# Two blocks' attention probabilities transposed in f32 where they are made, and the last gate product issued behind the first mixed rows

## The chip, the cores and the metric

The kernel runs on one core of one Trainium2 chip. The metric is the device time of one execution in microseconds (us); lower is better. The engines are called as the profile calls them: PE is TensorE (matmuls; PEld its weight loads), DVE is VectorE, ACT is ScalarE, POOL is GpSimd, and SP is the queue from which most DMAs are issued. Each engine runs its own instructions in order, and waits on semaphores for the others.

## The reference

One layer of a hybrid backbone over 2048 latent tokens of width 1024, with 256 context tokens. Cut to what matters here:

```python
def sink_softmax(logits, sink):
    m = jnp.maximum(jnp.max(logits, axis=-1, keepdims=True), sink)
    p = jnp.exp(logits - m)
    return p / (jnp.sum(p, axis=-1, keepdims=True) + jnp.exp(sink - m))
...
    h = rms_norm(x) * (1.0 + scale[:, None, :]) + shift[:, None, :]
    rq, rk, rv, rg, aq, ak, av, ag = project(h, w_in[l])
...
    ret_x, _, _ = retention_branch(rq, rk, rv, rg, log_gamma, ret_gn_w[l], s_fwd, s_bwd)
    att_x = merge_heads(windowed_gqa(aq, ak, av, cak, cav, att_sink[l])) * jax.nn.silu(ag)
    mixed = jnp.concatenate([ret_x, att_x], axis=-1) @ w_out[l]
    x = x + gate[:, None, :] * mixed
    return rms_norm(x) * final_norm_w
```

Retention has 4 heads of 128, in both directions, with a group norm and a SiLU gate (rg). Attention has 8 heads of 64 on 2 key/value heads: a block of 128 queries sees its own and the two neighbouring blocks of 128 keys and all 256 context keys, so a row of probabilities has 640 entries, 512 in the first and the last block, and one for the sink behind them.

## The kernel before

It has two phases. The first, up to about 688 us, makes all projections: for groups of 512 tokens, products of the weights and the normalised input, each split in a high and a low fp32r half (three products a tile). The last chunk is ag1 of the first token group (the rows "ag" of L343). The second phase goes over 16 blocks of 128 tokens, two steps a block (one for each key/value head, kv), 32 steps t in all. A step holds attention heads of the next step, retention, transposes and products of the present one, and pieces of the output projection. The tables STEPS, FIRST and WEAVE give the order in which the program writes them; a scheduler then orders each engine's instructions by its own estimate of when their inputs are there, in a window around that. `behind(i)` binds an instruction to come after instruction i. The first block's heads are woven into the last gate chunk by WEAVE (0 to 7 are heads, A and B the first transposes, a and b their products), and FIRST has what follows in step 0: its transposes T, the mixed rows Y (`ret_out`), and G (`last_gate`).

One attention head goes like this. PE makes the scores S (L759 and L763; there is one buffer for S, so the next head's scores wait until it is read). DVE adds the mask and takes the maximum (L767), puts the sink's column behind (L772) and prepares the bias (L773). ACT takes the exponential with the sum (L776). DVE takes the reciprocal of the sum (L785), POOL multiplies by it (L786). These work on a tile p of 641 columns, of which there are four, shared by all steps. Then SP issues a DMA that copies the row from p into tile pr (L790). pr holds the four heads of a step in fp32r, 640 columns each, and there are two of them.

For each 128 keys (kt), PE transposes the four heads of pr (L1200) against identr, the identity in fp32r, into a bank pt. ACT rounds pt to the high half phl (L1206), DVE subtracts for the low half (L1207), and PE multiplies both with the values into o (L1217). Block 0 has four kt, the others five, so a step has 16 or 20 transposes.

`gate_by_tanh` (L1233 to L1236) makes a gate: tanh on ACT, a scale by 0.5 on DVE or POOL, the product with the projection on DVE (L1235, tile gl), and a DMA to memory. `ret_out` (L1274 to L1279) transposes the retention rows (yt, against ident, the identity in f32), multiplies by the gate gr (L1276), and splits the result in mr, a cast (a helper's line, L113) and a subtraction (L1279); block 0 does both on DVE, the others on POOL. `proj` (L1290) is the output projection pz, from mr (weights wg0) and from the attention's rows ma (weights wg1).

Loads are issued on SP in the order of the program. Of these, `load_qkv` and `load_late` (tile xb) come behind the latest pr copy from block 2 on:

```python
            with behind(PE["copy"] if b > 1 else None):
                nc.sync.dma_start(QKV[b], d_qkv[b])
```

Of the kernel before, what the change touches and what calls it, by code (L numbers as in the profile page):

```python
# [8 lines left out]
F32 = mybir.dt.float32  # L9
F32R = mybir.dt.float32r  # L10
# [29 lines left out]
def tile_hymba(  # L40
# [49 lines left out]
    sink8 = const.tile([P, 8], F32, name="sink8")  # L90

    EPSV = (EPS, EPS * P)
    half4 = const.tile([P, 4], F32, name="half4")
    dve.memset(half4, -0.5)
    eps1 = const.tile([P, 1], F32, name="eps1")
    dve.memset(eps1, EPS)


# [589 lines left out]
    def load_qkv(b):  # L688
        if b < NB:
            QKV[b] = l2.tile([P, 3, RH, P], F32, tag="qkv", name=f"qkv{b}")  # L690
            with behind(PE["copy"] if b > 1 else None):
                nc.sync.dma_start(QKV[b], d_qkv[b])

    def load_st(b):
# [33 lines left out]
    def load_late(b):  # L728
        if b >= NB:
            return  # L730
        tiles_late(b)
        if b:
            nc.sync.dma_start(GA[b], d_g[b, :, 1])
        else:
            nc.sync.dma_start(GA[b][:, 0:2], d_g[b, :, 1, 0:2])
        with behind(PE["copy"] if b > 1 else None):
            nc.sync.dma_start(XB[b], xn[b * P : (b + 1) * P, :])


    def att_head(b, kv, j):  # L740
        slots = window(b)[0]
        nl = len(slots) * P
        n = nl + CTX
        o = 512 - nl
        h = 4 * kv + j
        ksel = {0: slice(0, 2), NB - 1: slice(0, 3, 2)}.get(b, slice(0, 3))
        m0 = mask_at(b)
        mk = C2["msk"][:, m0 : m0 + n // P].rearrange("p s t -> p (s t)")
        if j == 0:
            PB[(b, kv)] = (  # L750
                C2["pool"].tile([P, 4, 640], F32R, tag="pr", name=f"pr{b}_{kv}"),
                C2["pool"].tile([P, 3, 4], F32, tag="m4", name=f"m4{b}_{kv}"),
                [C2["pool"].tile([P, 641], F32, tag="pb", name=f"p{b}_{kv}_{i}", bufs=4) for i in range(4)],
            )
        _, m4, pbs = PB[(b, kv)]
        pb = pbs[j]
        psc = pS.tile([P, 1024], F32, tag="S", name=f"S{b}_{h}")
        for hl in range(2):
            i = pe.matmul(  # L759
                psc[:, o:512].rearrange("p (s t) -> p s t", t=P),  # L760
                AQ[b][:, h, :], C2["kwin"][:, kv, hl, ksel], start=(hl == 0), stop=(hl == 1),
            )
            pe.matmul(psc[:, 512:768], AQ[b][:, h, :], C2["kctx"][:, kv, hl], start=(hl == 0), stop=(hl == 1))  # L763
        PE["S"] = i

        with behind(PE["low"] if (b, kv) == (1, 0) else None):
            i = PE["max"] = dve.tensor_tensor_reduce(  # L767
                out=pb[:, 0:n], in0=psc[:, o : o + n], in1=mk, op0=ALU.add, op1=ALU.max,
                scale=1.0, scalar=-3e38, accum_out=m4[:, 0, j : j + 1],
            )  # L770
        with behind(i):
            dve.tensor_copy(pb[:, n : n + 1], sink8[:, h : h + 1])  # L772
        dve.tensor_scalar(  # L773
            m4[:, 1, j : j + 1], m4[:, 0, j : j + 1], -0.125, nsink[:, h : h + 1], op0=ALU.mult, op1=ALU.min
        )
        act.activation(  # L776
            pb[:, 0 : n + 1], pb[:, 0 : n + 1], AF.Exp, bias=m4[:, 1, j : j + 1], scale=0.125,
            accum_out=m4[:, 2, j : j + 1],
        )

    def att_norm(b, kv, j):
        n = len(window(b)[0]) * P + CTX
        pr_, m4, pbs = PB[(b, kv)]
        pb = pbs[j]
        dve.reciprocal(m4[:, 2, j : j + 1], m4[:, 2, j : j + 1])  # L785
        PE["norm"] = pool.tensor_scalar(  # L786
            pb[:, 0:n], pb[:, 0:n], m4[:, 2, j : j + 1], 0.0, op0=ALU.mult, op1=ALU.add
        )

        PE["copy"] = nc.sync.dma_start(pr_[:, j, 0:n].bitcast(F32), pb[:, 0:n])  # L790

    BANKS = {"o": 1, "z": 2, "t": 3}

# [400 lines left out]
    def att_t(b, kv, kt, weave=False):  # L1194
# [2 lines left out]

        with behind(PE.get("prod") if kt == 0 else None):
            for j in range(4):
                pe.transpose(ppt[:, j].bitcast(F32R), pb[:, j, kt * P : (kt + 1) * P], identr)  # L1200
        if weave:
            phl = [tmp(f"phl{kt}{x}", dt=F32R).rearrange("p (j t) -> p j t", t=P) for x in "hl"]
        else:
# [27 lines left out]
    def gate_by_tanh(t, idx, ps, eng):  # L1231

        act.activation(t, ps, AF.Tanh, scale=0.5)  # L1233
        eng.tensor_scalar(t, t, 0.5, 0.5, op0=ALU.mult, op1=ALU.add)
        dve.tensor_tensor(t, t, ps, op=ALU.mult)  # L1235
        act.dma_start(d_g[0:4, :, 1, idx, :].rearrange("b d t -> d b t"), t.rearrange("d (b t) -> d b t", b=4))  # L1236


# [31 lines left out]
    def ret_out(b):  # L1270
        sd = RT[b][1]
        pt = bank(f"yt{b}")
        for h in range(RH):
            pe.transpose(pt[:, h], sd[:, h], ident)  # L1274
        g = GR[b]
        dve.tensor_tensor(g, pt, g, op=ALU.mult)  # L1276
        MR[b] = s1.tile([P, 2, RH, P], F32R, tag="mr", name=f"mr{b}")
        rounded(MR[b][:, 0], g, "pool" if b else "dve")
        (pool if b else dve).tensor_tensor(MR[b][:, 1], g, MR[b][:, 0], op=ALU.subtract)  # L1279


    PZ = {}
# [212 lines left out]
```

## Time and profile before

| what | us |
|---|---|
| median of three timed runs | 1150.86 |
| lowest and highest of the three | 1150.78 and 1152.02 |
| the profiled execution, its own time | 1151.28 |
| its span, from the first to the last instruction | 1149.5 |
| mean granted clock of PE | 0.995 of full |
| DMAs pr<-p: count, median from issue to landing | 128 of them; the 112 of 320 KB take 3.0 |

The profile is of one execution. Rows of the timeline have the start, the duration, engine, line, operation, output and inputs, count, and in brackets the idle time ahead and what ended it. Rows of several windows have the window, then for each engine busy time and count, the granted clock (1.00 is full), the share of the DMA engines and GB/s. Buffer numbers are left out of names: pr stands for all pr tiles. Matmuls are pipelined: a row's duration overlaps the next one's, so the distance of two starts tells more than a duration.

### The profile page before, as it was taken

The page shows a single profiled execution, that of the slowest core. Times are in us where ns is not written, and L with a number is a line of the kernel's source. Part 1 is how long each engine was busy: PE and PEld are TensorE (multiplying, and loading weights), DVE is VectorE, ACT ScalarE, POOL GpSimd, SP SyncE. Part 2 cuts the span into 40 slices and gives each one's busy share as a digit, 9 for nine tenths or more (in the row PEclk, how much of TensorE's full clock was granted, in tenths as well). Part 3 has the DMA queues.
Part 4 walks back from the last instruction along what each step waited for, and adds up shares of the span by engine and source line. Part 5 has one row for each costly group of instructions (what it writes and reads, how often), then busy time and mean ns, then how long its engine had stood idle before and what let it go on. Part 6 is the DMA issues. An engine that isn't in the chain of part 4 may idle for free.

```text
span 1149.5 us, 18705 instructions
## 1 busy us (share of the span) xinstructions
PE 1121.1 (98%) x6317; PEld 959.8 (83%) x6318; DVE 800.2 (70%) x2029; ACT 467.6 (41%) x1030; POOL 330.7 (29%) x429
## 2 busy tenths in 40 slices
PE   8999999999999999999999998899999999999997
PEld 5877879989988889998888876788888888888885
DVE  7873994655664555656566456778888888888884
ACT  4444512332443002332111343555556655556563
POOL 0000020100011100002014333455555555555552
PEclk9999999999999999999999999999999999999999
DMA  9948883374675533543356378666666666666541
GB/s 340 335 145 263 296 279 119 120 255 136 203 234 170 146 103 88 170 133 97 115 181 195 94 207 269 199 230 231 227 233 228 228 228 225 228 227 227 188 147 65
DMA packets 158552, 224.32 MB, mean 195 GB/s; under 512 B 13300, under 2 KB 105204, under 8 KB 158327
## 3 DMA queue, kind: packets, MB, share of 16 engines
q1 hardware_dynamic: 142324, 214.95, 57.3%
q10 hardware_dynamic: 16130, 8.16, 2.4%
q8 instruction: 50, 0.82, 0.3%
q14 instruction: 48, 0.39, 0.1%
HBM read 130.13 MB, written 50.86 MB: 157 GB/s over the span
## 4 chain that ended last, share of the span: by engine, by line
PE 80%; DVE 7%; issue 5%; DMA 4%; ACT 2%; POOL 2%; SPq 0%; POOLq 0%; DVEq 0%; ACTq 0%
PE pz L1290 14%; PE ag L343 8%; PE rk L343 7%; PE rv L356 7%; PE o L1217 6%; PE aq L343 5%; PE rg L343 4%; PE S L759 4%; PE rq L343 4%; PE pt L1200 4%; PE S L763 2%; PE av L343 2%; PE ak L343 2%; PE u L472 2%; DVE wss L215 1%
## 5 line engine op out<-in xcount | busy, mean ns | idle before, releaser
L786 POOL TENSOR_SCALAR p<-p,m 128x640 f32<-128x640 f32 (+1 forms) x128 | 107.7, 842 | 107.0 <-DMA kwin<-d_k 46.3
L776 ACT ACTIVATE p<-p,m 128x641 f32<-128x641 f32 (+1 forms) x128 | 104.6, 817 | 75.9 <-DVE m L773 45.8
L1207 DVE TENSOR_TENSOR phl<-pt,phl 128x512 fp32r<-128x512 f32 x154 | 104.7, 681 | 18.7 <-ACT phl L1206 18.4
L767 DVE CUSTOM_DVE_ANT_0 p<-S,msk 128x640 f32<-128x640 f32 (+1 forms) x128 | 102.2, 798 | 10.1 <-PE S L763 6.5
L1206 ACT ACTIVATE phl<-pt 128x512 fp32r<-128x512 f32 x154 | 90.9, 592 | 43.8 <-PE pt L1200 37.7
L1290 PE MATMUL pz<-wg0h,mr 128*128 128x512 f32 x256 | 98.2, 406 | 1.9 <-DVE mr L113 1.9
L1290 PE MATMUL pz<-wg1h,ma 128*128 128x512 f32 x256 | 99.0, 413 | 0.2
L759 PE MATMUL S<-kwin,aq 128*128 128x384 f32 (+1 forms) x256 | 85.1, 352 | 3.1 <-DVE m L767 2.0
L1200 PEld LDWEIGHTS pt<-identr,pr 128*128 128x128 f32 x624 | 68.2, 141 | 15.7 <-DMA pr<-p 3.0
L448 ACT ACTIVATE vw<-v,wdec 128x128 fp32r<-128x128 f32 x128 | 43.7, 394 | 84.8 <-DVE v L461 84.8
L1200 PE MATMUL pt<-identr,pr 128*128 128x128 f32 x624 | 72.2, 240 | 3.3 <-DMA pr<-p 2.8
L1217 PE MATMUL o<-phl,vwin 128*128 128x512 f32 x180 | 72.3, 429 | 2.9 <-DVE phl L1207 2.1
L763 PE MATMUL S<-kctx,aq 128*128 128x256 f32 x256 | 71.4, 282 | 0.0
L1290 PEld LDWEIGHTS pz<-wg0h,mr 128*128 128x128 f32 x256 | 48.0, 188 | 10.4 <-DVE mr L113 2.2
L759 PEld LDWEIGHTS S<-kwin,aq 128*128 128x128 f32 x256 | 48.1, 188 | 7.8 <-DVE m L767 3.0
L1290 PEld LDWEIGHTS pz<-wg1h,ma 128*128 128x128 f32 x256 | 48.0, 188 | 7.8 <-POOL ma L1268 1.0
L763 PEld LDWEIGHTS S<-kctx,aq 128*128 128x128 f32 x256 | 48.4, 189 | 2.7
L1290 PE MATMUL pz<-wg0l,mr 128*128 128x512 f32 x128 | 50.5, 394 | 0.0
L1290 PE MATMUL pz<-wg1l,ma 128*128 128x512 f32 x128 | 50.5, 394 | 0.0
L1261 ACT ACTIVATE ob<-o 64x512 f32<-64x512 f32 x32 | 19.1, 596 | 63.9 <-PE o L1217 63.9
L450 DVE SCALAR_TENSOR_TENSOR vw<-v,wdec,vw 128x128 fp32r<-128x128 f32 x128 | 40.4, 360 | 6.7 <-ACT vw L448 6.7
L1217 PEld LDWEIGHTS o<-phl,vwin 128*128 128x128 f32 x180 | 32.4, 187 | 14.3 <-DVE phl L1207 5.8
(444 smaller groups left out, 3057.2 us busy)
## 6 DMA issues: line engine op xcount, KB each, us to landing
pr<-p SPq DMA_DIRECT2D x112, 320.0 KB, 3.0
wss<-in_wss SPq DMA_DIRECT2D x32, 512.0 KB, 5.9
qkv<-d_qkv SPq DMA_DIRECT2D x15, 768.0 KB, 5.9
aq<-d_aq SPq DMA_DIRECT2D x64, 128.0 KB, 3.2
xb<-in_xn SPq DMA_DIRECT2D x16, 512.0 KB, 4.0
out<-xb SPq DMA_DIRECT2D x31, 256.0 KB, 2.6
st<-d_st SPq DMA_DIRECT2D x15, 512.0 KB, 3.5
d_g<-g ACTq DMA_DIRECT2D x28, 256.0 KB, 2.8
```

Of the source, the lines that this page charges most:

```text
L343: pe.matmul(ps, w[:, a, k, c0 : c0 + P], ht[b][:, k, :], start=(k == 0 and i == 0), stop=(k == NK - 1 and i == 2),)
L356: pe.matmul(ps, ht[a][:, k, t * P : (t + 1) * P], w[:, b, k, :], start=(k == 0 and i == 0), stop=(k == NK - 1 and i == 2),)
L759: i = pe.matmul(psc[:, o:512].rearrange("p (s t) -> p s t", t=P), AQ[b][:, h, :], C2["kwin"][:, kv, hl, ksel], start=(hl == 0), stop=(hl = ...
L763: pe.matmul(psc[:, 512:768], AQ[b][:, h, :], C2["kctx"][:, kv, hl], start=(hl == 0), stop=(hl == 1))
L767: i = PE["max"] = dve.tensor_tensor_reduce(out=pb[:, 0:n], in0=psc[:, o : o + n], in1=mk, op0=ALU.add, op1=ALU.max, scale=1.0, scalar=-3e3 ...
L776: act.activation(pb[:, 0 : n + 1], pb[:, 0 : n + 1], AF.Exp, bias=m4[:, 1, j : j + 1], scale=0.125, accum_out=m4[:, 2, j : j + 1],)
L786: PE["norm"] = pool.tensor_scalar(pb[:, 0:n], pb[:, 0:n], m4[:, 2, j : j + 1], 0.0, op0=ALU.mult, op1=ALU.add)
L1200: pe.transpose(ppt[:, j].bitcast(F32R), pb[:, j, kt * P : (kt + 1) * P], identr)
L1206: PE["phl"] = act.activation(phl[0], ppt, AF.Copy)
L1207: PE["low"] = dve.tensor_tensor(phl[1], ppt, phl[0], op=ALU.subtract)
L1217: pe.matmul(PO[kv], vt, PH[kt][hl], start=(kt == 0 and hl == 0), stop=(kt == nkt - 1 and hl == 1))
L1290: PE["prod"] = pe.matmul(PZ[n2], m[:, a, k % RH, :], WG[k // 4][c][:, k % 4, s], start=(k == 0 and i == 0), stop=(k == NK - 1 and i == 2),)
```

## The change

There are three parts. For blocks 0 and 1 (DIRECT = 2), pr is an f32 tile, the softmax works in place on its rows, and there is no p tile and no DMA copy: 16 DMAs of SP fall away. The 72 transposes of these blocks (32 in block 0, 40 in block 1) read f32 and the f32 identity. From block 2 on the route is as before, but pr has rows of 641 columns in all blocks, so its rows are 2564 bytes apart and not 2560. The loads of qkv and xb are bound to a copy only once there is one, so those of blocks 2 and 3 (qkv) and 2 (xb) are free. Two small constants come into one tile (half5). And the product of the gate is bound behind the last instruction of block 0's mixed rows (`PE["mr"]`), which exists only when the last gate is made.

```diff
-    half4 = const.tile([P, 4], F32, name="half4")
+    half5 = const.tile([P, 5], F32, name="half5")
+    half4, eps1 = half5[:, 0:4], half5[:, 4:5]
...
-    eps1 = const.tile([P, 1], F32, name="eps1")
...
-            with behind(PE["copy"] if b > 1 else None):
+            with behind(PE.get("copy")):
                 nc.sync.dma_start(QKV[b], d_qkv[b])
...
-        with behind(PE["copy"] if b > 1 else None):
+        with behind(PE.get("copy")):
             nc.sync.dma_start(XB[b], xn[b * P : (b + 1) * P, :])
+
+    DIRECT = 2
...
         if j == 0:
+            pr_ = C2["pool"].tile([P, 4, 641], F32 if b < DIRECT else F32R, tag="pr", name=f"pr{b}_{kv}")
             PB[(b, kv)] = (
-                C2["pool"].tile([P, 4, 640], F32R, tag="pr", name=f"pr{b}_{kv}"),
+                pr_,
                 C2["pool"].tile([P, 3, 4], F32, tag="m4", name=f"m4{b}_{kv}"),
-                [C2["pool"].tile([P, 641], F32, tag="pb", name=f"p{b}_{kv}_{i}", bufs=4) for i in range(4)],
+                [
+                    pr_[:, i]
+                    if b < DIRECT
+                    else C2["pool"].tile([P, 641], F32, tag="pb", name=f"p{b}_{kv}_{i}", bufs=4)
+                    for i in range(4)
+                ],
             )
...
-        PE["copy"] = nc.sync.dma_start(pr_[:, j, 0:n].bitcast(F32), pb[:, 0:n])
+        if b >= DIRECT:
+            PE["copy"] = nc.sync.dma_start(pr_[:, j, 0:n].bitcast(F32), pb[:, 0:n])
...
-                pe.transpose(ppt[:, j].bitcast(F32R), pb[:, j, kt * P : (kt + 1) * P], identr)
+                x = pb[:, j, kt * P : (kt + 1) * P]
+                if b < DIRECT:
+                    pe.transpose(ppt[:, j], x, ident)
+                else:
+                    pe.transpose(ppt[:, j].bitcast(F32R), x, identr)
...
-        dve.tensor_tensor(t, t, ps, op=ALU.mult)
+        with behind(PE.get("mr")):
+            dve.tensor_tensor(t, t, ps, op=ALU.mult)
...
-        (pool if b else dve).tensor_tensor(MR[b][:, 1], g, MR[b][:, 0], op=ALU.subtract)
+        PE["mr"] = (pool if b else dve).tensor_tensor(MR[b][:, 1], g, MR[b][:, 0], op=ALU.subtract)
```

Each engine has the same instructions as before but for SP's 16 copies and the transposes' type; their order differs between about 671 us and the end of block 1's steps. In the rows of order below, numbers behind names are those of buffers, and differ between the programs; the changed kernel's lines are 9 to 15 higher.

At block 0's y products, PE now has head 5's scores and three products of the last gate (ag) ahead of the first y product, and three more ag between the last y product and the first transposes; before, head 5's scores and these products stood behind the first four transposes, which followed y at once. On DVE the masks of heads 4 and 5 stood among and behind the group statistics of y (L837, L838); now both stand ahead of them, and head 6's is the first behind. ACT, behind block 0's y (first), before (pt_0_0 and pt_0_1 feed phl0h and phl1h, p or pr with m is the exponential, gl the gate's tanh):

```order
L825 ACTIVATE first<-y_6350 128x512
L1236 DMA d_g<-gl_6297 128x4x128
L776 ACTIVATE p_1_0_6305,m_1_6304<-p_1_0_6305,m_1_6304 128x513
L853 ACTIVATE first<-first,mod 128x128 x2
L776 ACTIVATE p_1_1_6306,m_1_6304<-p_1_1_6306,m_1_6304 128x513
L853 ACTIVATE first<-first,mod 128x128 x2
L1206 ACTIVATE phl0h<-pt_0_0_6386 128x512
L1206 ACTIVATE phl1h<-pt_0_1_6410 128x512
```

and after:

```order
L835 ACTIVATE first<-y_6335 128x512
L1220 ACTIVATE phl0h<-pt_0_0_6371 128x512
L863 ACTIVATE first<-first,mod 128x128 x4
L785 ACTIVATE pr_1_6294,m_1_6295<-pr_1_6294,m_1_6295 128x513
L1220 ACTIVATE phl1h<-pt_0_1_6394 128x512
L1247 ACTIVATE gl_6486<-ag_6293 128x512
```

phl0h has moved ahead of the rows L853 (now L863), phl1h stands behind all four of them and an exponential.

DVE, the end of step 0, before (S_7 is the last head of block 0, gl the last gate, gr and mr the mixed rows):

```order
L767 ISA p_1_3_6308,m_1_6304<-S_7_6430,msk 128x512
L767 ISA m_1_6304 128x1
L772 COPY p_1_3_6308<-sink_83 128x1
L773 TENSOR_SCALAR m_1_6304<-m_1_6304,nsink 128x1
L1235 TENSOR_TENSOR gl_6503<-gl_6503,ag_6302 128x512
L785 RECIPROCAL m_1_6304<-m_1_6304 128x1
L1276 TENSOR_TENSOR gr_6216<-yt_6488,gr_6216 128x512
L113 CAST mr_6494<-gr_6216 128x512
L1279 TENSOR_TENSOR mr_6494<-gr_6216,mr_6494 128x512
```

and after:

```order
L776 ISA pr_1_6294,m_1_6295<-S_7_6414,msk 128x512
L776 ISA m_1_6295 128x1
L1221 TENSOR_TENSOR phl1l<-pt_0_1_6394,phl1h 128x512
L781 COPY pr_1_6294<-sink_83 128x1
L782 TENSOR_SCALAR m_1_6295<-m_1_6295,nsink 128x1
L794 RECIPROCAL m_1_6295<-m_1_6295 128x1
L1291 TENSOR_TENSOR gr_6215<-yt_6471,gr_6215 128x512
L113 CAST mr_6477<-gr_6215 128x512
L1294 TENSOR_TENSOR mr_6477<-gr_6215,mr_6477 128x512
L1250 TENSOR_TENSOR gl_6486<-gl_6486,ag_6293 128x512
```

The gate product has gone from ahead of gr to behind mr, and the low half of the second transposes (phl1l) stands between the last mask and gr.

PE, block 1's first transposes, before (pt_0_0 to pt_0_2 are the first three kt of kv 0, S_5 and S_6 scores of kv 1, ma and wg1 the attention's part of block 0's projection):

```order
L1290 MATMUL pz_1_6670<-wg1h,ma_6554 128x512
L1200 MATMUL pt_0_0_6739<-identr,pr_0_6535 128x128
L1200 MATMUL pt_0_1_6749<-identr,pr_0_6535 128x128
L1200 MATMUL pt_0_2_6785<-identr,pr_0_6535 128x128
L1200 MATMUL pt_0_0_6739<-identr,pr_0_6535 128x128
L1200 MATMUL pt_0_1_6749<-identr,pr_0_6535 128x128
L1200 MATMUL pt_0_2_6785<-identr,pr_0_6535 128x128
L759 MATMUL S_5_6724<-kwin,aq_6211 128x384
L763 MATMUL S_5_6724<-kctx,aq_6211 128x256
```

and after, from head 5's last scores on:

```order
L772 MATMUL S_5_6695<-kctx,aq_6210 128x256
L1305 MATMUL pz_1_6646<-wg1h,ma_6533 128x512
L1305 MATMUL pz_1_6646<-wg1l,ma_6533 128x512
L1305 MATMUL pz_1_6646<-wg1h,ma_6533 128x512
L1212 MATMUL pt_0_0_6709<-ident,pr_0_6518 128x128 x4
L1212 MATMUL pt_0_1_6719<-ident,pr_0_6518 128x128 x4
L768 MATMUL S_6_6737<-kwin,aq_6210 128x384
```

Before, all 24 products of wg1 stand ahead of the first of these rows; after, six stand ahead of head 5's scores, three more ahead of the transposes, and the others between the transposes and products that follow. The transposes of one kt stand together.

## The prediction

> **What bounds the kernel now.** I read the page first, then the waits of the matmul engine by stretch, then its timeline in the stretch where it waits.
>
> ```profile
> span 1149.5 us, 18705 instructions
> PE 1121.1 (98%) x6317; PEld 959.8 (83%) x6318; DVE 800.2 (70%) x2029; ACT 467.6 (41%) x1030; POOL 330.7 (29%) x429
> ```
>
> PE is busy 98% of the span, so time comes only from PE's own work or from the 28 us in which it idles. The waits of PE between 660 and 765 us, where every moved instruction lies (us in total, times, longest), and then from 765 us to the end:
>
> ```profile
> PE pt L1200 <- DMA pr<-p: 2.8, 2, 1.5
> PE S L759 <- DVE m L767: 2.0, 2, 1.3
> PE pz L1290 <- DVE mr L113: 1.9, 1, 1.9
> PE S L759 <- DVE p L772: 1.1, 1, 1.1
> PE o L1217 <- ACT phl L1206: 0.8, 1, 0.8
> PE o L1217 <- DVE phl L1207: 0.7, 2, 0.4
> PE s L813 <- DMA qkv<-d_qkv: 0.6, 1, 0.6
> PE pt L1200 <- ACT first L825: 0.6, 1, 0.6
> PE y L822 <- DMA st<-d_st: 0.4, 1, 0.4
> PE y L822 <- POOL qd L806: 0.4, 1, 0.4
> ...
> PE o L1217 <- DVE phl L1207: 1.4, 1, 1.4
> ```
>
> These ten rows sum to 11.3 us; after 765 us there are 1.4 us in 385. So what PE gains before 765 us should reach the end undiminished, and the hunt is over 11 us. Only 2.8 of them wait for a pr copy itself: 1.3 in block 1 and 1.5 in block 2, and the second copy stays. The rest must come from the order that the edits set free.
>
> **The change, part by part.** I replay three pieces and compare each with its length in the profiled run.
>
> *A. From block 0's y products (674.20) to the first projection (pz).*
>
> ```profile
> 674.20 0.38 PE L821 MATMUL y<-sfw,first 128*128 128x128 f32 x2
> 679.37 0.39 PE L759 MATMUL S<-kwin,aq 128*128 128x256 f32 x1 [1.27 <-DVE m L767]
> 691.65 0.50 PE L1290 MATMUL pz<-wg0h,mr 128*128 128x512 f32 x1 [1.90 <-DVE mr L113]
> ...
> 679.00:680.00 1.00, 0.63 (x4) 0.63 (x5) 0.66 (x6) 0.35 (x1) 0.25 (x1) 0.84 0.60 188
> 680.00:683.00 3.00, 3.00 (x11) 2.31 (x10) 1.07 (x6) 2.05 (x7) 1.74 (x3) 0.50 0.01 3
> 688.00:692.00 4.00, 2.10 (x18) 1.80 (x17) 2.85 (x9) 2.39 (x5) 1.58 (x3) 1.00 0.85 260
> ```
>
> The piece takes 17.45 us. Of this 0.56 (for ACT's first) + 1.27 + 1.90 = 3.7 are waits, and 680 to 683 us ran at a granted clock of 0.50 (the column ahead of the last two), which lost 3.0 x 0.5 = 1.5 us. Each wait also hides the tail of the matmul before it, some 0.17 us (eight pt, quoted below, last 0.81 while the next row starts after 0.64). That leaves 17.45 - 3.7 - 1.5 - 0.5 = 11.7 us of work. The new order (told with the change) puts head 5's scores and three gate products ahead of the y products and three more behind them, and head 4's mask stands ahead of the group statistics on DVE. So the waits of 0.56 and 1.27 go, and with them the gap that preceded the slow clock. What is late next is phl1h, on ACT:
>
> ```profile
> 681.42 0.88 ACT L853 ACTIVATE first<-first,mod 128x128 f32<-128x128 f32 x2 [0.95 <-DVE mod L846]
> 684.66 0.60 ACT L1206 ACTIVATE phl1h<-pt 128x512 fp32r<-128x512 f32 x1 [0.33 <-PE pt L1200]
> ...
> 689.53 0.69 DVE L1235 TENSOR_TENSOR gl<-gl,ag 128x512 f32<-128x512 f32 x1 [1.08 <-POOL gl L1234]
> 690.14 0.16 DVE L785 RECIPROCAL m<-m 128x1 f32<-128x1 f32 x1
> 690.21 0.67 DVE L1276 TENSOR_TENSOR gr<-yt,gr 128x512 f32<-128x512 f32 x1
> 690.92 0.68 DVE L113 CAST mr<-gr 128x512 fp32r<-128x512 f32 x1
> ```
>
> ACT now runs all four L853 rows (2 x 0.88) and one exponential (about 0.9 with its accumulator) ahead of phl1h; L853 waits for the statistics and POOL's powers as before. The y products end 1.2 us later (one head's scores and three gate products stand ahead of them), and a mask of some 0.8 is gone from between the statistics: L853 starts at 681.42 + 1.2 - 0.8 = 681.8, ends at 683.5, the exponential at 684.4, phl1h at 685.0. PE reaches the product that reads it at about 683.5 and waits 1.6. The last gate product ends near 685.5 instead of 688.0. Behind it the gl product no longer holds up gr: DVE sat idle 1.08 us for POOL, then multiplied, before gr could start. gr now waits only for tanh, the last exponential and its reciprocal (0.8 + 0.9 + 0.15: 687.35); gr and its cast (0.67 + 0.68) end at 688.7, and PE, done at 687.7, waits 1.0. The f32 transposes add 0.6 (below). The new length is 11.7 + 1.6 + 1.0 + 0.6 = 14.9, a gain of 2.55; I take **2.5**. It would be 0.5 if both new waits came out 1 us longer, 3.0 with 0.5 less of them. The loads behind (s 0.64, y 0.44) I leave as they are: their issues no longer queue behind copies on SP, so they move with PE.
>
> *B. Block 1, first half (709 to 728).*
>
> ```profile
> 715.28 0.63 PE L1200 MATMUL pt<-identr,pr 128*128 128x128 f32 x6
> 717.05 0.41 PE L759 MATMUL S<-kwin,aq 128*128 128x384 f32 x1 [1.15 <-DVE p L772]
> 718.81 0.44 PE L759 MATMUL S<-kwin,aq 128*128 128x384 f32 x1 [0.72 <-DVE m L767]
> 720.68 0.51 PE L1217 MATMUL o<-phl,vwin 128*128 128x512 f32 x1 [0.77 <-ACT phl L1206]
> ```
>
> Before these waits PE ran 24 pz products (wg1) in one piece, and then had nothing to lay over heads 5, 6 and 7 and the first phl. Now the 24 (5.5 us) stand between the same instructions. The five waits here are 1.15 + 0.72 + 0.77 + 0.7 = 3.34. Head 5's scores come after six products (1.4 us) while the mask of head 4 takes some 2 us with what DVE has ahead of it, so I leave 0.75 there, and 0.4 for the f32 transposes: a gain of **2.2**, between 0.9 (if the chain of softmax steps on DVE, ACT and POOL is itself the limit, and takes back most of it) and 3.8 (no wait left, and the hidden tails too).
>
> *C. Block 1, second half (728 to 737).*
>
> ```profile
> 735.01 0.28 PE L1200 MATMUL pt<-identr,pr 128*128 128x128 f32 x1 [1.29 <-DMA pr<-p]
> 730.71 0.97 POOL L786 TENSOR_SCALAR p<-p,m 128x640 f32<-128x640 f32 x1
> 731.70 0.50 SPq L790 DMA_DIRECT2D pr<-p  x1
> ```
>
> The row that PE waits for was normalised by 731.7; the copy took the 3.3 us after it. Without the copy it is ready 2.0 us before PE stood there (735.01 - 1.29 = 733.7). So 1.29 goes; the 0.4 for qd stays; f32 costs 0.4: a gain of **0.9**, up to 1.7 with qd's wait gone and f32 free. The wait of 1.5 in block 2 stays, since its chain moves with PE.
>
> *Transposes in f32.* None of pt is f32 in the trace; pk (L432, f32 against the same identity) is the nearest row, and a run of eight pt:
>
> ```profile
> 188.85 1.03 PE L432 MATMUL pk<-ident,m_rk 128*128 128x128 f32 x8
> 189.64 0.48 PE L356 MATMUL rv<-w_brv,h3h 128*128 128x256 f32 x2
> ...
> 862.60 0.81 PE L1200 MATMUL pt<-identr,pr 128*128 128x128 f32 x8
> 863.24 0.42 PE L759 MATMUL S<-kwin,aq 128*128 128x384 f32 x1
> ```
>
> Eight take 0.79 in f32 and 0.64 in fp32r: 0.02 us more each, times 72 (32 in block 0, 40 in block 1) = 1.4 us, the 0.6 + 0.4 + 0.4 above; at best nothing. The Trainium skill, "FP8 and Floating Point Precision", section "TensorE Precision Notes", says that true FP32 takes four passes through the array. By it the sum would be that of rival 4 below; the trace does not bear it out for transposes (0.79 against 0.64).
>
> *The wider pr tile.* All later blocks copy into rows 2564 bytes apart, not 2560, so three of four start off a 32-byte grid. No row shows such a copy. I cost it at nothing, since of the 112 copies that stay PE waits for one. The bound on the other side is rival 2.
>
> The sum is 2.5 + 2.2 + 0.9 = 5.6 us. The profiled run took 1151.28 us (0.4 above the median of 1150.86), so the forecast is **1145.7 us**. Half4 and eps1 in one tile cost nothing; the freed qkv and xb loads are worth the s and y waits at most (1.0 us), and I count 0.
>
> **Rivals.**
>
> *1. The waits are only replaced.* The softmax of each head is a chain DVE, ACT, DVE, POOL; one score buffer ties PE to it. If chain and loads set the pace, A gives 0.5, B 0.9, C 0.3: 1149.6 us. For it: five of the ten waits name DVE or ACT. Against: the engines of the chain have room there (DVE idle 1.08 us ahead of one gl product).
>
> *2. Slower: the off-grid copies.*
>
> ```profile
> pr<-p SPq DMA_DIRECT2D x112, 320.0 KB, 3.0
> 846.03 0.51 SPq L790 DMA_DIRECT2D pr<-p  x1
> 849.65 0.54 PE L1200 MATMUL pt<-identr,pr 128*128 128x128 f32 x4
> ```
>
> In a settled block the fourth copy is issued 3.6 us before its first transpose and takes 3.0: 0.6 us of slack. If copies took 4.2, each of 14 blocks would wait 0.6, 8.4 in all: 1154.1 us. Above 4.0 us the gain of 5.6 is eaten up. The Trainium skill, "DMA: Bandwidth & Descriptors", section "How a descriptor splits into AXI transactions", has a start off the 256-byte grid cost a partial transaction; for a row of 2560 bytes that is an estimated 1 beat in 80, far inside the slack. No run here shows it yet.
>
> *3. A second clock drop.* PE idles 1.6 + 1.0 us between 683 and 689. Before, 676 to 680 dropped the clock, while 688 to 692, as idle (2.10 of 4 busy), did not. If one falls, 1.5 us come back: 1147.2 us. The Trainium skill, "TensorE: Matmul & The Clock Gate", section "What's actually happening", has free-running windows of about 3.4 us, so that the phase decides; the 3.0 us at 0.50 agree.
>
> *4. f32 transposes at four times the cost.* 0.24 us more each instead of 0.02: 72 x 0.22 = 15.9 us, 1161.6 us. pk speaks against it.
>
> **How the numbers follow.** Forecast 0.60; waits replaced 0.18; second clock drop 0.12; off-grid copies 0.07; dear transposes 0.03. A measurement tells this kernel from no change by about 0.2%, 2.3 us, so faster means below 1148.6: the forecast, the clock drop and 0.04 of rival 1, 0.76. Same takes 0.14 of rival 1; slower the last two, 0.10. The low end has A at 3.0, B at 3.8 and C at 1.7 (with qd's wait gone and f32 free): 8.5, and 0.5 from loads, about 1142.3. The high end is 1150.0, most of rival 1; what is left out holds 0.2.
>
> **What would show it.** In the changed profile: pt<-DMA only in block 2; no stretch at 0.50 near 680; a wait of o for phl1h on ACT of about 1.6; the first pz near 689; the wg1 products spread over 709 to 722; L1212 in f32 at about 0.1 us a piece; copies still at 3.0 us, and no waits after 765. A first pz later than 691, or PE waits per block behind copies, would prove it wrong.

## The result and the profile after

| | us |
|---|---|
| before, median of four runs beside the changed kernel | 1151.44 (1150.78 to 1153.94) |
| changed, median of four runs | 1138.37 (1137.71 to 1141.22) |
| changed / before, 95% interval | 0.9887, 0.9864 to 0.9910 |
| profiled execution of the changed kernel, its own time | 1138.54 |

The changed kernel is faster by 13.07 us in these medians; 5.6 were forecast, and 1138.37 lies below the low end of the range. Timed again later, the same kernel came out 10.28 us below the kernel before beside it (ratio 0.9909), so the gain in medians is 10 to 13 us.

The page of the changed kernel, its span, busy times and the copies that are left (count, KB each, median us from issue to landing):

```profile
span 1136.8 us, 18646 instructions
PE 1119.6 (98%) x6317; PEld 958.4 (84%) x6318; DVE 799.6 (70%) x2029; ACT 467.3 (41%) x1030; POOL 329.3 (29%) x429
...
pr<-p SPq DMA_DIRECT2D x104, 320.0 KB, 3.0
```

PE's busy time fell by 1.5 us and the span by 12.7, so 11.2 us of the gain were time in which PE idled. PE's waits from 660 to 765 us (total, times, longest), and behind the dots from 765 us to the end:

```profile
PE o L1231 <- ACT phl1h L1220: 1.0, 1, 1.0
PE pz L1305 <- DVE mr L113: 0.7, 1, 0.7
PE S L768 <- DVE m L776: 0.5, 1, 0.5
PE o L1231 <- ACT phl L1220: 0.2, 1, 0.2
...
PE o L1231 <- DVE phl L1221: 1.4, 1, 1.4
PE pt L1214 <- DMA pr<-p: 0.3, 1, 0.3
```

Before 765 us, ten rows with 11.3 us have become four with 2.4. The first two are the waits that the prediction put in place of the old ones; no load and no copy is left among the four.

To see where the time went I cut both timelines at the same instructions of PE: block 0's first scores, the first pz, the first transposes of block 0's second half, the first wg1 product, the first transposes of block 1's second half, the next wg1 product, and block 2's first wg0 product.

| piece | start before | start after | length before | length after | gain | forecast |
|---|---|---|---|---|---|---|
| 1: first scores to first pz (A) | 663.78 | 661.53 | 27.87 | 24.49 | 3.38 | 2.5 |
| 2: to block 0's second transposes (loads) | 691.65 | 686.02 | 9.44 | 8.06 | 1.38 | 0 |
| 3: to wg1 | 701.09 | 694.08 | 8.15 | 8.70 | -0.55 | 0 |
| 4: to block 1's second transposes (B and the head of C) | 709.24 | 702.78 | 24.01 | 19.56 | 4.45 | 2.2 and 0.9 with piece 5 |
| 5: to the next wg1 (rest of C) | 733.25 | 722.34 | 11.71 | 10.66 | 1.05 | |
| 6: to block 2's first wg0 | 744.96 | 733.00 | 15.12 | 13.48 | 1.64 | 0 |
| all six | | | 96.30 | 84.95 | 11.35 | 5.6 |

From there to PE's last matmul it is 381.92 us before and 382.86 after; over the fourteen profiles of this study this stretch is 381.7 to 383.5, whatever the edit. The changed kernel also starts the first scores 2.25 us earlier, which is not the change's doing. A window of the kernel before (busy time and count of PE, PEld, DVE, ACT, POOL; granted clock; share and GB/s of the DMAs), in which PE was busy without a break:

```profile
235.00:239.00 4.00, 4.00 (x21) 3.76 (x21) 2.75 (x5) 1.21 (x3) 0.00 (x0) 0.62 0.34 93
```

The changed kernel's profile has 1.00 there. But a second profile of one variant of the changed kernel (rows_late, below) has the low clock too and starts its first scores at 663.94, while its first profile has not and starts them at 660.86. So I compare kernels by the six pieces, and times by medians.

The same pieces 4 to 6 by engine, first B's own stretch up to block 1's first wg0 product, then the rest of C, then block 2; the kernel before:

```profile
709.24:728.05 18.81, 15.32 (x84) 11.84 (x83) 12.56 (x37) 9.00 (x20) 7.09 (x11) 1.00 0.54 191
728.05:744.96 16.91, 15.25 (x97) 13.20 (x95) 12.13 (x39) 7.83 (x16) 10.02 (x12) 1.00 0.66 198
744.96:760.08 15.12, 13.66 (x84) 11.63 (x83) 12.06 (x36) 8.24 (x19) 7.77 (x9) 1.00 0.69 248
```

and the changed kernel:

```profile
702.78:717.68 14.90, 14.29 (x85) 11.89 (x84) 11.98 (x36) 8.16 (x18) 8.73 (x11) 1.00 0.56 186
717.68:733.00 15.32, 15.32 (x96) 13.41 (x95) 11.76 (x39) 8.64 (x18) 7.27 (x11) 1.00 0.54 179
733.00:746.48 13.48, 13.48 (x84) 11.60 (x83) 12.06 (x36) 8.25 (x19) 7.78 (x9) 1.00 0.60 211
```

PE idled 18.81 - 15.32 = 3.49, then 1.66 and 1.46 us; now 0.61, 0 and 0. That is 6.0 of the 7.14 us that these stretches gained (50.84 - 43.70). The other 1.1 are recorded as busy time, and nearly all of it lies in the first stretch (15.32 - 14.29 = 1.03). One part is tails: a matmul's recorded end overlaps the next start, and where PE waits, the tail of some 0.17 us counts as busy. Six of the eight waits here are gone, which makes 1.0, but the dearer transposes take 40 x 0.02 = 0.8 of it back. The rest is rows of the kernel before that were stretched without a listed wait:

```profile
711.75 0.77 PE L1290 MATMUL pz<-wg1h,ma 128*128 128x512 f32 x2
...
722.31 0.72 PE L1274 MATMUL yt<-ident,sd 128*128 128x128 f32 x2
```

Six wg1 products from the first row on take 1.90 us (to 713.65), where the six ahead of them took 1.36 (from 710.39), and the two transposes of the second row take 0.72, where the two ahead of them took 0.38: 0.9 us together. DVE, ACT and POOL do the same work in less time, so their own speed was not the limit.

The forecast's two new waits, in the timeline of the changed kernel (PE, then ACT, then DVE):

```profile
682.50 0.50 PE L1231 MATMUL o<-phl1h,vwin 128*128 128x512 f32 x1 [1.01 <-ACT phl1h L1220]
686.02 0.49 PE L1305 MATMUL pz<-wg0h,mr 128*128 128x512 f32 x1 [0.66 <-DVE mr L113]
...
679.60 1.65 ACT L863 ACTIVATE first<-first,mod 128x128 f32<-128x128 f32 x4 [1.89 <-DVE mod L856]
681.16 0.71 ACT L785 ACTIVATE pr<-pr,m 128x513 f32<-128x513 f32 x1
681.87 0.58 ACT L1220 ACTIVATE phl1h<-pt 128x512 fp32r<-128x512 f32 x1
...
684.81 0.69 DVE L1291 TENSOR_TENSOR gr<-yt,gr 128x512 f32<-128x512 f32 x1
685.54 0.43 DVE L113 CAST mr<-gr 128x512 fp32r<-128x512 f32 x1
686.61 0.68 DVE L1250 TENSOR_TENSOR gl<-gl,ag 128x512 f32<-128x512 f32 x1
```

With the 2.25 us of the earlier start added, L863 begins at 681.85 where 681.8 was forecast, phl1h at 684.12 where the forecast had 684.4, and the first pz at 688.27 where it had about 689. The gate product (L1250) stands behind the cast that PE waits for.

And the transposes, eight in f32, then eight in fp32r, each with the row behind them:

```profile
706.16 1.03 PE L1212 MATMUL pt<-ident,pr 128*128 128x128 f32 x8
706.95 0.42 PE L768 MATMUL S<-kwin,aq 128*128 128x384 f32 x1
...
735.67 0.80 PE L1214 MATMUL pt<-identr,pr 128*128 128x128 f32 x8
736.30 0.43 PE L768 MATMUL S<-kwin,aq 128*128 128x384 f32 x1
```

From start to start they take 0.79 and 0.63 us: 0.02 us more for each f32 transpose, as forecast from pk.

### The profile page after: what moved, and what is told of

It is laid out like the page before. It is cut to its first block, busy times and chain, and to the rows that moved or that the text cites. A ratio compares the mean times of both kernels' runs of the same rounds, so it can differ in the third digit from the quotient of the medians.

```text
span 1136.8 us, 18646 instructions
## 1 busy us (share of the span) xinstructions
PE 1119.6 (98%) x6317; PEld 958.4 (84%) x6318; DVE 799.6 (70%) x2029; ACT 467.3 (41%) x1030; POOL 329.3 (29%) x429
## 4 chain that ended last, share of the span: by engine, by line
PE 81%; DVE 6%; issue 5%; DMA 4%; ACT 2%; POOL 2%; POOLq 0%; ACTq 0%; DVEq 0%
PE pz L1305 13%; PE rv L356 8%; PE rk L343 8%; PE ag L343 7%; PE o L1231 6%; PE aq L343 5%; PE rg L343 4%; PE rq L343 4%; PE S L768 4%; PE pt L1214 3%; PE S L772 2%; PE u L472 2%; PE av L343 2%; PE ak L343 2%; DMA pr<-p 1%
## 5 line engine op out<-in xcount | busy, mean ns | idle before, releaser
L795 POOL TENSOR_SCALAR p<-p,m 128x640 f32<-128x640 f32 (+1 forms) x112 | 95.2, 850 | 86.5 <-DMA kwin<-d_k 46.7
L785 ACT ACTIVATE p<-p,m 128x641 f32<-128x641 f32 (+1 forms) x112 | 92.3, 824 | 62.2 <-DVE m L782 40.5
L776 DVE CUSTOM_DVE_ANT_0 p<-S,msk 128x640 f32<-128x640 f32 (+1 forms) x112 | 90.2, 806 | 3.1 <-PE S L772 1.3
L1214 PEld LDWEIGHTS pt<-identr,pr 128*128 128x128 f32 x552 | 59.8, 140 | 11.3 <-DMA pr<-p 0.6
L1214 PE MATMUL pt<-identr,pr 128*128 128x128 f32 x552 | 62.9, 240 | 0.3 <-DMA pr<-p 0.3
L1231 PE MATMUL o<-phl,vctx 128*128 128x512 f32 x128 | 43.8, 404 | 0.0
```

The source lines that it names most:

```text
L776: i = PE["max"] = dve.tensor_tensor_reduce(out=pb[:, 0:n], in0=psc[:, o : o + n], in1=mk, op0=ALU.add, op1=ALU.max, scale=1.0, scalar=-3e3 ...
L785: act.activation(pb[:, 0 : n + 1], pb[:, 0 : n + 1], AF.Exp, bias=m4[:, 1, j : j + 1], scale=0.125, accum_out=m4[:, 2, j : j + 1],)
L795: PE["norm"] = pool.tensor_scalar(pb[:, 0:n], pb[:, 0:n], m4[:, 2, j : j + 1], 0.0, op0=ALU.mult, op1=ALU.add)
L1214: pe.transpose(ppt[:, j].bitcast(F32R), x, identr)
L1231: pe.matmul(PO[kv], vt, PH[kt][hl], start=(kt == 0 and hl == 0), stop=(kt == nkt - 1 and hl == 1))
```

## The experiments

My first theory gave the gain to waits that fall away with the copies and with the gate product's place; its rivals were that the new order on PE does it without the missing copies, and that part of it is the clock or chance. The first kernels each take one part of the change alone. All ratios are against the kernel before on the same chip, with 95% intervals; "pieces" are the six above, 96.30 us before and 84.95 after.

**gate_only.** The kernel before with the gate product behind mr:

```diff
-        dve.tensor_tensor(t, t, ps, op=ALU.mult)
+        with behind(PE.get("mr")):
+            dve.tensor_tensor(t, t, ps, op=ALU.mult)
```

> The kernel before with the last gate's product behind the mixed rows and nothing else. Theory (the gain is the f32 route's, the gate's part is small): gr starts when the last exponential and its reciprocal allow, about 0.6 us earlier than 690.21, the first pz near 691.0, time 0 to 1 us below before. Rival (the gate product is the main part): the first pz 3 us or more earlier and 3 us or more off the time.

Measured: 1148.19 us against 1150.21, ratio 0.9981 (0.9968 to 0.9995). The median is 2.0 us lower, more than the 0 to 1 expected. The profiled execution was the slowest of the twelve (1151.27 us), so it shows more loss than most had: piece 1 is shorter by 1.23 us, but the pieces add up to 96.33, and what was gained was lost again behind it, where the granted clock fell to half:

```profile
718.00:725.00 7.00, 6.42 (x26) 5.02 (x27) 5.09 (x16) 5.43 (x12) 1.83 (x3) 0.53 0.56 194
749.00:752.00 3.00, 3.00 (x11) 2.41 (x11) 2.30 (x8) 3.00 (x8) 0.80 (x1) 0.52 0.60 207
```

Alone, this part is worth 0.6 to 3.7 us (0.9995 to 0.9968 of 1150.21), well under the whole.

**no_gate.** The changed kernel without that binding:

```diff
-        with behind(PE.get("mr")):
-            dve.tensor_tensor(t, t, ps, op=ALU.mult)
+        dve.tensor_tensor(t, t, ps, op=ALU.mult)
```

> The changed kernel with the gate's product unbound again. Theory: the product, ready at 684.6 in the changed profile, goes ahead of gr (684.81) and holds it and the first pz up by 0.5 us: 0.3 to 1 us above the changed kernel, 12 us below before. Rival (the gate product is the main part): 3 us or more above the changed kernel.

Measured: 1139.87 us, 0.9908 (0.9891 to 0.9924). Piece 1 is 25.20 instead of 24.49, all else within 0.1. The wait for mr doubled, since DVE again sits idle for POOL ahead of gl, and gr stands behind it (waits of PE, then DVE's timeline):

```profile
PE pz L1304 <- DVE mr L113: 1.4, 1, 1.4
...
686.89 0.69 DVE L1249 TENSOR_TENSOR gl<-gl,ag 128x512 f32<-128x512 f32 x1 [1.07 <-POOL gl L1248]
```

So within the change the gate's place is worth 0.7 us of the 11.35 in the pieces.

**wide_only.** The kernel before with half5 and rows of 641:

```diff
-                C2["pool"].tile([P, 4, 640], F32R, tag="pr", name=f"pr{b}_{kv}"),
+                C2["pool"].tile([P, 4, 641], F32R, tag="pr", name=f"pr{b}_{kv}"),
```

> The kernel before with the two constants in one tile and pr rows of 641, copies and fp32r transposes everywhere. It tests the layout alone: the tiles of the first phase lie 32 bytes lower, copies start off the 32-byte grid. Theory (layout costs and gains nothing; the 2.25 us by which block 0's first scores came earlier in the changed profile are chance, a clock drop near 237 us and loads): within 0.2% of before, copies at 3.0 us. Rival (the shifted tiles make the first phase faster): 2 us or more below before, block 0's first scores at 661.5 instead of 663.8. Rival of the prediction (off-grid copies are dear): copies at 4 us or more and slower by 5 us or more.

Measured: 1150.17 us, 0.9999 (0.9987 to 1.0011); copies at 3.0 us. **narrow_rows** is the reverse, the changed kernel with rows 640 apart from block 2 on:

```diff
+            if b >= DIRECT:
+                pr_ = pr_.rearrange("p j n -> p (j n)")[:, 0:2560].rearrange("p (j n) -> p j n", n=640)
```

> The changed kernel with rows of 640 columns in pr from block 2 on (the same tile, the rows 2560 bytes apart). Theory: the same time as the changed kernel within 0.2%, copies at 3.0 us. Rival (off-grid copies cost something that the gain hides): 1 us or more below the changed kernel, copies shorter than 3.0.

Measured: 1137.91 us, 0.9894 (0.9876 to 0.9913); copies at 3.0, pieces 84.94. The layout costs nothing either way; rival 2 is dead.

**f32_only.** The kernel before with f32 pr tiles and f32 transposes in blocks 0 and 1, but with its p tiles and all its copies:

```diff
-                C2["pool"].tile([P, 4, 640], F32R, tag="pr", name=f"pr{b}_{kv}"),
+                C2["pool"].tile([P, 4, 640], F32 if b < 2 else F32R, tag="pr", name=f"pr{b}_{kv}"),
...
+                if b < 2:
+                    pe.transpose(ppt[:, j], x, ident)
```

> The kernel before with pr of blocks 0 and 1 in f32 and their transposes in f32, but p tiles and all 128 copies kept. Theory (working in place is what frees the order; f32 itself costs 0.02 us a transpose): 0 to 2 us above before, PE still waits for copies and masks for 6 us or more between 660 and 765. Rival (the scheduler's new order is a matter of the transposes' type): 5 us or more below before.

Measured: 1145.15 us against 1151.17, 0.9952 (0.9934 to 0.9969). My theory missed here: no wait was taken away by hand, and 6 us went. The pieces add up to 90.22, 6.1 less than before. From the second half of block 0 on the scheduler had placed other rows: block 1's scores and copies stand earlier, the wg1 products still in one run. The waits of 660 to 765 us are 5.4 in all, and the one for block 2's copy has gone (the 0.2 that is left on a copy is block 1's):

```profile
PE pz L1294 <- DVE mr L113: 1.7, 1, 1.7
PE S L759 <- DVE p L772: 1.2, 1, 1.2
PE S L759 <- DVE m L767: 1.1, 2, 0.8
...
PE pt L1202 <- DMA pr<-p: 0.2, 1, 0.2
```

**order_only.** To test order by itself, the kernel before with block 0's wg1 products bound behind the latest scores, type and copies untouched:

```diff
+            with behind(PE["S"] if b == 0 and k >= RH else None):
                 PE["prod"] = pe.matmul(
```

> The kernel before (p tiles, copies, fp32r) with block 0's 24 products of wg1 bound behind the latest scores, which gives PE the changed kernel's order in block 1's first half and leaves the rest. Theory (the order is what gains there, not the missing copies): from the first wg1 product to block 1's second transposes 20 to 21 us (24.0 before, 19.6 in the changed kernel), 3 to 5 us below before. Rival (without the copies gone the softmax chain sets the pace): the piece stays above 23, less than 1 us gained.

Measured: 1143.32 us against 1149.89, 0.9943 (0.9929 to 0.9956), so 6.6 us with all copies and tiles kept. Neither expectation held whole: piece 4 stayed above 23 us (23.14, and not 19.56), as the rival had it, but far more than 1 us was gained. The pieces add up to 90.31, 6.0 less than before. Of this, 2.0 lie in pieces 1 and 2 (27.18 and 8.11 us), ahead of the first bound product, where PE, DVE, ACT and POOL run the same rows in the same order as before. These 2.0 are chance: the half clock near 680 and the two waits for loads happened not to come. That leaves 4.0 us for the order, 1.64 of it in piece 6 (13.48, as in the changed kernel). PE, DVE and the granted clock in piece 4:

```profile
709.79 0.45 PE L759 MATMUL S<-kwin,aq 128*128 128x384 f32 x1 [3.22 <-DVE m L767]
...
708.90 0.82 DVE L767 CUSTOM_DVE_ANT_0 p<-S,msk 128x640 f32<-128x640 f32 x1 [1.66 <-DMA pr<-p]
...
711.00:714.00 3.00, 2.78 (x15) 2.19 (x13) 1.48 (x7) 1.67 (x4) 1.28 (x2) 0.50 0.29 109
```

Read from the second row up: DVE's mask can't write its p tile before a copy has read it out; PE's next scores wait for the mask; and behind the gap PE runs 3 us at half clock. So in the new order the shared p tiles hold the chain in this piece, and working in place takes that away.

**direct1.** The changed kernel with DIRECT = 1, so block 1 goes through p tiles and copies again:

> The changed kernel with only block 0 in place (DIRECT = 1); block 1 copies as before. Theory (the gain is local to the block that works in place): the piece from block 0's first scores to block 1's first transposes takes about 32.5 us as in the changed kernel (37.3 before), block 1's pieces about as long as before, time 4 to 7 us below before. Rival (the gain comes from block 0 alone, later pieces follow from it): 10 us or more below before.

Measured: 1142.99 us, 0.9930 (0.9913 to 0.9947). That is 8.2 us below before, more than the 4 to 7 expected. Pieces 1 and 2 are as in the changed kernel (24.50 and 8.07), but block 1's pieces 4 and 5 take 31.8 us where before they took 35.7. Against the changed kernel pieces 4 to 6 are longer by 3.4 in all, 1.8 of it in piece 6, where block 2's wait is back (the longest of these):

```profile
PE pt L1214 <- DMA pr<-p: 2.2, 2, 1.6
```

**late_xb.** Why is that wait gone in the changed kernel? The edit frees block 2's load xb, which was bound behind a copy. SP's rows around the last two of the four copies differ. The changed kernel:

```profile
726.61 0.34 SPq L737 DMA_DIRECT2D xb<-in_xn  x1
727.05 1.31 SPq L680 DMA_DIRECT2D kwin<-d_k  x2
728.89 2.19 SPq L800 DMA_DIRECT2D pr<-p  x2
731.14 0.58 SPq L692 DMA_DIRECT2D qkv<-d_qkv  x1
```

and the kernel before:

```profile
741.84 0.48 SPq L790 DMA_DIRECT2D pr<-p  x1
742.42 0.53 SPq L737 DMA_DIRECT2D xb<-in_xn  x1
743.04 0.46 SPq L790 DMA_DIRECT2D pr<-p  x1
...
749.46 0.62 PE L1200 MATMUL pt<-identr,pr 128*128 128x128 f32 x5 [1.46 <-DMA pr<-p]
```

There the load xb (512 KB) was issued 0.6 us ahead of the fourth copy, and PE got its row 749.46 - 743.04 = 6.4 us after the copy's issue. late_xb is the changed kernel with xb of block 2 behind the third copy again:

```diff
+        if (b, kv, j) == (2, 0, 2):
+            with behind(PE["copy"]):
+                nc.sync.dma_start(XB[2], xn[2 * P : 3 * P, :])
```

> The changed kernel with the load of block 2's xb issued behind the third copy of block 2's first step, where it stood before, and nothing else moved. Theory (before, this 512 KB load shared the DMA engines with the fourth copy, which took 6.4 us, and made PE wait 1.5 us in block 2; the change moved the load): the fourth copy takes 5 us or more again, PE waits 0.8 to 2 us for it at the first transposes of block 2, 0.8 to 2 us above the changed kernel. Rival (the wait went because the softmax chain runs earlier): no wait, the same time.

Measured: 1138.94 us, 0.9894 (0.9878 to 0.9910). The fourth copy, issued behind the load, and the transposes that wait for it:

```profile
730.34 0.53 SPq L804 DMA_DIRECT2D xb<-in_xn  x1
731.41 0.50 SPq L801 DMA_DIRECT2D pr<-p  x1
...
737.12 0.63 PE L1218 MATMUL pt<-identr,pr 128*128 128x128 f32 x5 [0.27 <-DMA pr<-p]
```

The trace has the fourth copy's own time from issue to landing; the changed kernel, late_xb and the kernel before:

```profile
pr<-p SPq DMA_DIRECT2D x1, 320.0 KB, 3.0
...
pr<-p SPq DMA_DIRECT2D x1, 320.0 KB, 5.7
...
pr<-p SPq DMA_DIRECT2D x1, 320.0 KB, 6.4
```

So the load does lie in the copy's way. In the kernel before PE came to the copy's rows 749.46 - 1.46 - 743.04 = 5.0 us behind its issue; a copy of 3.0 us would have made no wait there. In late_xb PE waits only 0.27 for it, and piece 6 grows by 0.43, not by 1.64 (0.8 to 2 were expected): the copy lands 0.7 us sooner than the one before, and PE comes 5.4 us behind its issue. The other kernels agree on the pattern: gate_only, wide_only and direct1 have xb 0.6 us ahead of the fourth copy, which takes 6.6 to 6.7 us, and waits of 1.6 to 1.7; order_only and f32_only issue it 1.7 and 1.0 us ahead of a copy, their fourth copies take 3.3 and 3.9, and they don't wait in block 2. The distance alone does not set the copy's time, though: it is 1.1 us in late_xb (5.7) and 1.0 in f32_only (3.9).

**idle_copies.** The changed kernel, with 16 copies added that nobody reads, from pr into p tiles:

```diff
+        if b < DIRECT:
+            idle = C2["pool"].tile([P, 641], F32, tag="pb", name=f"idle{b}_{kv}_{j}", bufs=4)
+            nc.sync.dma_start(idle[:, 0:n], pr_[:, j, 0:n])
```

> The changed kernel with 16 copies added back that nothing reads: each row of pr of blocks 0 and 1 is copied to a p tile when it is normalised. It brings back the waits on SP's queue and the DMA traffic, not PE's wait for a copy. Theory (part of the gain is that loads no longer queue behind copies): qkv, st and xb come later, the piece from the first pz to block 1's first transposes goes from 8.1 towards 9.4, a wait of block 2 for its fourth copy returns, 1.5 to 4 us above the changed kernel. Rival (the queue does not matter): within 0.5 us of the changed kernel.

Measured: 1140.60 us, 0.9927 (0.9909 to 0.9944), 1.0 us above the changed kernel timed beside it (1139.61, below); the two intervals overlap. Pieces 86.74, 1.8 us more: 0.3 in pieces 4 and 5 together (eight score products moved from 4 to 5) and 1.4 in piece 6. The theory missed: piece 2 is 8.35 and not near 9.4, and no wait for a copy came back in block 2, though xb is issued 0.4 us ahead of the fourth copy and that takes 5.6, since block 2's first transposes stand later. What PE waits for in piece 6, 0.6 of the 1.4, is a mask that DVE does late, behind a wait for POOL (DVE, then PE):

```profile
734.60 0.17 DVE L859 SCALAR_TENSOR_TENSOR ra<-mv,ra 128x4 f32<-128x4 f32 x1 [2.39 <-POOL ra L118]
...
735.88 0.45 PE L768 MATMUL S<-kwin,aq 128*128 128x384 f32 x1 [0.59 <-DVE m L776]
```

So the 1.8 us come with 16 more copies and the order that they bring; that SP's queue or the DMA engines cost them isn't shown.

**rows_late.** The largest wait that is left is that for phl1h. This kernel writes block 0's row scalings (L863) behind it:

```diff
-        "y": lambda: (ret_values(0), ret_moments(0), ret_norm(0), ret_rows(0, range(RH)), ret_state(0)),
+        "y": lambda: (ret_values(0), ret_moments(0), ret_norm(0), ret_state(0)),
+        "r": lambda: ret_rows(0, range(RH), PE["phl"]),
```

> The changed kernel with block 0's four row scalings on ACT written behind phl1h. Theory (PE's wait of 1.0 for phl1h is the rows' and the exponential's on ACT, and the chain behind it sets the first pz): that wait goes, the first pz comes 0.7 to 1.5 us earlier after block 0's first scores (24.5 in the changed profile), 0.7 to 1.5 us below the changed kernel. Rival (the last mask and exponential set the first pz anyway): less than 0.5 us.

Measured: 1139.81 us, 0.9896 (0.9876 to 0.9915). The wait for phl1h is gone, and piece 1 is 23.97, 0.5 shorter where 0.7 to 1.5 were expected, but the time tells nothing. The changed kernel and this one were then timed again side by side.

> The changed kernel once more, as control beside the others. Theory (half-clock stretches between 660 and 765 us need the stalls of the old order; when they fall is chance): 84.5 to 85.5 us from block 0's first scores to block 2's first wg0 product, no half-clock stretch there, 1138 to 1139 us. Rival (the missing half clock was chance too): a stretch at 0.50 there, 1.5 us or more longer.

> The kernel with block 0's row scalings behind phl1h once more, beside the changed kernel of the same call. Theory (it saves the 0.6 us that its profile showed between block 0's first scores and block 2's first wg0 product): 0.3 to 1 us below the changed kernel. Rival: the same or slower.

Measured: 1139.61 us, 0.9909 (0.9892 to 0.9927) for the changed kernel, and 1139.45, 0.9908 (0.9892 to 0.9924) for rows_late; pieces 84.98 and 84.57. The 0.4 us can be read in the profile and not in the time. No version here beats the changed kernel measurably.

## Why the prediction was right in direction and too small

**Right.** The bound was read correctly: only PE's waits between 660 and 765 us mattered, and what was gained there reached the end. The waits for phl1h and mr came where they were forecast; the wg1 products are spread from 702.8 to 717; the f32 transposes cost 0.02 us each; the copies stayed at 3.0 us. Rivals 2 and 4 are dead (wide_only, and the 0.79 us for eight transposes). So is rival 3 for this kernel: neither profile of it has a half clock between 660 and 765 us. Rival 1 is dead as well, since ten waits of 11.3 us became four of 2.4. That the half clock near 680 is gone was forecast too, from the waits ahead of it, but order_only and wide_only have those waits and no half clock there: that the profile before had it was chance, and no run shows that the change removed it.

**A, forecast 2.5, measured 3.38.** The mechanism held, and three terms were mis-sized. The waits were 1.01 and 0.66 instead of 1.6 and 1.0 (0.9 us together): the exponential held ACT for 0.71 us (681.16 to 681.87) where 0.9 was taken, and PE waited only 0.48 us for the cast (685.54 to 686.02) where 0.68 was. Of the 0.6 for f32 transposes only 0.3 belong here, as 16 of block 0's 32 stand in piece 3. And the tails behind the two new waits, 0.34, were not added. With these the sum closes: 11.7 + 1.01 + 0.66 + 0.34 + 0.3 = 14.0, and the piece takes 24.49 - 10.42 (the stretch of the kernel before ahead of y, 663.78 to 674.20) = 14.07. The 1.5 for the half clock fits this sum because the waits went too. With the old waits kept it costs less: order_only runs the same instructions up to the first pz without it in 27.18 us instead of 27.87, so 0.7; the rest was covered by waits that it shortened.

**"The loads behind I leave as they are", 0, measured 1.38.** Both waits went (0.64 + 0.44, and their tails). But order_only has the old instructions here, and passes them in 8.11 us with no wait for a load. From issue to first use, qkv took 688.47 to 695.57 = 7.1 us before and 6.3 in order_only. In the old order it is the landing that decides; every kernel with the new order and without added edits in this stretch takes 7.96 to 8.07. In wide_only, with the old order, no load is waited for either; its 9.44 us hold a half clock from 688 to 692 instead. So this term is partly chance of the one profile. The changed kernel also has one wg0 product less in this piece (11 for 12), 0.23 us, and one more in piece 3.

**B, forecast 2.2, measured 3.91 (709.24 to 728.05 against 702.78 to 717.68).** PE's idle time fell by 2.9, close to the forecast's 3.34 - 0.75 = 2.6. This term is mis-sized because it counted idle time alone: PE's busy time fell by 1.03 as well, though the f32 transposes added 0.4. Three tails net are 0.5 (five waits gone, two left), which A had deducted and B named for the upper bound alone, and the stretched rows shown above are 0.9.

**Piece 3, 0, measured -0.55.** f32_only pays 0.3 for the 16 f32 transposes here, which the forecast had booked under A; the wg0 product from piece 2 is 0.23.

**C, forecast 0.9, measured 1.59 (728.05 to 744.96 against 717.68 to 733.00).** The wait of 1.29 went as forecast. The 0.37 for qd, which the forecast kept, went too, as its upper bound allowed, and the tails of both are 0.34.

**"The wait of 1.5 in block 2 stays, since its chain moves with PE", 0, measured 1.64.** This step failed, and with it the price of the freed loads ("worth the s and y waits at most (1.0 us), and I count 0"). The chain doesn't move as a piece: xb, freed by the edit, came 2.3 us ahead of the last two copies, and the fourth copy took 3.0 us instead of 6.4. The wait of 1.46 and its tail of 0.17 are the 1.64. The forecast rested on the rows of PE, ACT and DVE; those of SP around block 2, where xb's new place stands, were left out. The copy's time alone is enough to take the wait away; late_xb, which puts xb back, gives back 0.43 only, since PE came later against the copy there.

The six differences (0.9 + 1.4 - 0.55 + 1.7 + 0.7 + 1.6) make 5.75, which is 11.35 - 5.6.

**What the gain is made of** was also drawn too simply. The forecast had the order follow from the missing copies. With all copies kept, order_only has 6.0 us less in the pieces and f32_only 6.1, by reorderings that overlap: both clear block 2. But some 2 us of each lie in pieces 1 and 2, in order_only ahead of anything that its edit moves, so 4.0 are the order's. The changed kernel's other 5.4 us below order_only (90.31 - 84.95) are 3.6 in piece 4, where order_only's wait of 3.22 and the half clock behind it show the shared p tiles at work, and 2.7 in piece 1, less 0.9 elsewhere. Of the 2.7 the gate binding is 0.7. The other 2.0 come with the new rows around block 0's y; no run has this order with p tiles and copies, so order and in-place tiles are not told apart there.

**What stays open.** Which of f32_only's moved rows are worth what it gained, and why the type moves them, was not tried. Nor can I split the difference of the medians into order and clock: profiles of the old order lost one to three stretches to the half clock between 660 and 765 us (wide_only 715 to 722 at 0.54, for one) while f32_only lost none, so the median before has an amount of it that a single profile doesn't tell.

## What to carry to other kernels

When an edit changes what a scheduler sees (a type, a buffer, a DMA), compare the order of every queue in all stages behind it, the DMA queue above all; here a load that the edit had freed moved by a few rows and cleared a wait of 1.5 us in a block whose copies the edit keeps. Where a wait is priced as gone, take its hidden tail with it each time, and add one for each new wait: here some 0.17 us each. Before an edit gets the credit, run its order alone with everything else kept, and see whether what was gained lies behind the first row that moved: here 6.0 of 11.35 us seemed to be the order's, and 2.0 of them were not.

## What the runs showed of the hardware

- **Half clock without recorded idle time.** The kernel before ran 235 to 239 us at a granted clock of 0.62 on average with PE busy 4.00 of 4, and 231 to 235 was busy 4.00 of 4 as well. Four profiles of fourteen have this stretch (0.59 to 0.80), two kernels of the old order and two of the new, and these four start their first scores at 663.8 to 663.9 us where the other ten start at 660.9 to 663.4. Behind gaps it came too: 3 us at 0.50 behind a wait of 3.22, 7 us at 0.53. The Trainium skill, "TensorE: Matmul & The Clock Gate", section "What's actually happening", has free-running windows of 3413 ns and the slow state after an idle one. The 3 and 7 us are near one and two such windows; the stretch near 235 us has no idle window ahead of it in the trace. Its busy time just ahead is of a special kind, though: in all fourteen profiles PE runs four products of a single row (L209, pc<-room,ones, 1.98 us, in the kernel before from 233.33 to 235.24). Whether such products count as work for the clock was not tried.
- **A 320 KB copy behind a 512 KB load** took 5.7 us from issue to landing in late_xb, 6.4 in the kernel before and 6.6 to 6.7 in three more, and 3.0 in the changed kernel, where the load was issued earlier; but only 3.9 in f32_only, with the load 1.0 us ahead.
- **Rows 2564 bytes apart** cost the copies nothing: a median of 3.0 us in wide_only as before, ratio 0.9999 for the layout alone.
